# A convolution's written order: taps of the second half ahead of the first half's mean, tap matrices and evictions later

## The chip, the cores and the metric

The kernel runs on one core of one Trainium2 chip. The metric is the device time of one execution in microseconds (us). Five engines take part: TensorE (PE in the profile; PEld is its loading of weights), VectorE (DVE), ScalarE (ACT), GpSimd (POOL), which here mainly issues loads of weights, and SyncE (SP), which issues most DMA transfers.

## The reference

A decoder trunk of two layers for one sequence of 512 positions and 1024 channels. Layer 0 mixes with a state-space group and an attention group, layer 1 with a convolution module; each mixer and each MLP is followed by a residual addition and a layer norm. What matters here is the convolution module of layer 1:

```python
def conformer_conv(x, w_pw1, b_pw1, w_dw, b_dw, ln_g, ln_b, w_pw2, b_pw2):
    h = x @ w_pw1 + b_pw1                       # 1024 -> 2048
    val, gate = jnp.split(h, 2, axis=-1)
    h = val * jax.nn.sigmoid(gate)
    h = lax.conv_general_dilated(               # causal, 31 taps, each channel by itself
        h, w_dw[:, None, :], window_strides=(1,), padding=[(CONV_SIZE - 1, 0)],
        dimension_numbers=('NWC', 'WIO', 'NWC'), feature_group_count=CONV_WIDTH) + b_dw
    h = jax.nn.silu(layer_norm(h, ln_g, ln_b))  # norm over the 1024 channels
    return h @ w_pw2 + b_pw2
...
x = layer_norm(DEEPNORM_ALPHA * x + mix, ln1_g[layer], ln1_b[layer])
ffn = sqrelu_mlp(x, ffn_w1[layer], ffn_b1[layer], ffn_w2[layer], ffn_b2[layer])
```

## The kernel before, in words

Activations lie with channels on the partitions: eight channel tiles of 128 by 512 positions. A float32 product is three products on TensorE (high by high, low by high, high by low), so every operand is split into `whi`, `wlo` or the like: ScalarE makes the high part and VectorE the low one. Layer norms go over partitions: a product with a matrix of `ones` (`colmean`, L959) gives a mean or a variance to all partitions. They go by halves of the sequence, positions 0 to 255 and 256 to 511.

The convolution module follows layer 0's MLP and its norm (tiles `xbh`, `xbl`; the first products with them are named `pl`). For each of the eight tiles j, `glu_tile` makes the two products (`pv`, `pg`), ScalarE the sigmoid (`csg`), VectorE the gated tile `hp` (L398). Then come the 31 taps. Tiles 0 to 2 have them all on VectorE (`taps_dve`: one `scalar_tensor_tensor` each, in turn into `cy` and `cz`, which an addition at the end joins). Tile 3 has 11 taps on TensorE and 19 on VectorE; ScalarE opens `cy` and `cz`. Tiles 4 to 7 have all on TensorE: `weights_4` makes matrices W from the tap weights on VectorE (L1184), `spread` copies `hp` four times, shifted, into tiles `H` by DMA (L1192, on SP's queue), and `taps_128` multiplies (`cw`, L1200, four column groups at once). ScalarE then evicts the result into `cy` with the bias. The sum over tiles, for the mean, grows in `sc` (`LN.add`), one addition by VectorE for each tile and half.

The norm over channels is in three steps: `centred` (the mean `mpc`, subtraction on VectorE, squares `sqc` on ScalarE, their sums on VectorE), `scaled_var` (the variance `vpc`, then the reciprocal root on ScalarE and three steps on VectorE), and `normalised` (for each tile: a product on VectorE, Silu on ScalarE, and the split into `csh` by ScalarE and `csl` by VectorE). What follows is the tail: the products with `w_pw2` (`tld`, 24 of them for a tile and half, in `Tail.run`), added to the residual `X` by VectorE, with the sum `sd` for the next norm. After it come that norm (`mpd`, `vpd`, `xdh`, `xdl`) and the first products of the last MLP (`fl`).

What sets the order is a list written by hand, `CONV_ORDER` (L39). Each word is a step: a letter, the tile, and a third character for the half (0 or 1) where a step does only one.

- `g` is `glu_tile`, `u` its value product alone, `h` the copies, `w` the tap matrices, `p` taps on TensorE
- `v` is a part of a tile's taps on VectorE; `PARTS` says that a whole tile has 10 parts and a half has 4
- `f` is eviction and sum of a tile that TensorE has done
- `x` scales the residual, `M`, `Q` and `n` are the three steps of the norm (`n` for two tiles at a time)
- `t` is one tile of the tail

`run` executes the words, and `in_order` chains the instructions that each issues on TensorE, VectorE and ScalarE to those before, so that these three engines run in the order of the list. DMA issues are not chained; SP's and POOL's queues keep the order in which the program was recorded. Tail tiles that the list doesn't name are issued by `tail_norm_lead` after it, and the scheduler places them.

Of the kernel before, what the change touches and what calls it, by code (L numbers as in the profile page):

```python
# [35 lines left out]
CONV = 31  # L36
PE_BLOCKS = (0, 0, 0, 3, 8, 8, 8, 8)
PARTS = (10, 4)
CONV_ORDER = ("w3 w4 g0 v0 v0 g1 v0 v0 v0 v0 v0 g2 v0 w5 v0 v0 v1 g3 h3 v1 v1 v1 v1 g4 h40 h41 v1 v1 x0 v1 w6 v1 v1 g5 h50 w7 p3 p40 h51 "  # L39
              "v20 v20 v20 v20 g6 h60 f40 v30 p50 v30 f50 g70 h70 p41 h61 f41 v30 v30 p60 f60 p70 f70 u71 M0 g71 h71 v21 p51 Q0 p61 f51 p71 f61 "  # L40
              "n0 n0 n0 n0 f71 v21 t v21 t v21 v31 t v31 t v31 v31 t M1 Q1 n1 n1 n1 n1").split()
SPLIT_TILES = 1
ROOM = 288
HP = (0, 1, 2, 3, 0, 1, 4, 5)
# [159 lines left out]
def kernel(ctx: ExitStack, tc: tile.TileContext, a: dict, out: bass.AP):  # L204
# [806 lines left out]
    class Tail:  # L1011
# [7 lines left out]
        def run(self, n):  # L1019

            nj = KT // len(self.xk)
            for _ in range(n):
                h, j = divmod(self.done, KT)
                c0, c1 = HALVES[h]
                ps = nps(f"tl{self.ln.n}{c0}{j}")
                last = gemm(ps, self.ws[j // nj], slice((j % nj) * P, (j % nj + 1) * P), self.xk, c0, c1)
                x = X[j][:, c0:c1]
                if self.bias is None:
                    tt(x, ps[:, c0:c1], x, ALU.add)
                else:  # L1030
                    stt(x, ps[:, c0:c1], self.bias[:, j : j + 1], x, ALU.add, ALU.add)
                self.ln.add(j, X, c0, c1)
                self.done += 1
            return last
# [283 lines left out]

    split_at = CONV_ORDER.index("t")
    run(CONV_ORDER[:split_at])  # L1320

    def the_rest(t):
        run(CONV_ORDER[split_at:], t)

# [197 lines left out]
```

## Time and profile before

| | |
|---|---|
| median of 3 runs (lowest, highest) | 1161.32 us (1161.25, 1162.76) |
| profiled execution, its own time | 1162.09 us |
| its span, first to last instruction | 1160.4 us |
| mean granted TensorE clock | 0.992 |
| TensorE busy | 1130.9 us, 97% |
| VectorE busy | 810.6 us, 70% |
| ScalarE busy | 538.1 us, 46% |
| DMA | 175.35 MB, mean 151 GB/s |

The convolution lies between about 632 us (the end of the norm ahead of it) and 813 us (the first `fl` behind its tail). Times in a row of the profile are in us from the span's start. A row of the timeline has the start, the length, the engine, the line, the operation with its tiles and shapes, how many, and in brackets how long the engine was idle before it and who ended that. Rows of a stretch give the length, then for each engine the busy time and the number of instructions, then the granted TensorE clock (1.00 is full speed), the DMA engines' share and GB/s.

### The profile page before, as it was taken

To read this page: it belongs to the slowest core of one execution; us is meant where nothing else is said; L and a number is where in the kernel's file an instruction comes from. 1 tells how busy PE (TensorE), PEld (TensorE's weight loads), DVE (VectorE), ACT (ScalarE), POOL (GpSimd) and SP (SyncE) were. 2 spreads that over 40 slices of the span, in tenths; PEclk is the share of its full clock that TensorE was granted. 3 is DMA by queue.
4 is the path that set the end of the run, shared out by engine and by line. 5 is a ranking of instruction groups with operands and counts; after the bars stand their busy time and mean duration, and the time that the engine had idled before them with its cause. 6 is when DMAs were issued, how large, how long until landed. Compare 5 with 4: busy or idle time off the path is not lost.

```text
span 1160.4 us, 16446 instructions
## 1 busy us (share of the span) xinstructions
PE 1130.9 (97%) x6460; PEld 949.7 (82%) x6460; DVE 810.6 (70%) x1408; ACT 538.1 (46%) x814; POOL 39.7 (3%) x77
## 2 busy tenths in 40 slices
PE   9999999999999999999999999988999999999997
PEld 7777777799888888888899877688988888888885
DVE  7998875498646545645548887697795958588337
ACT  6956778345525424524403221515674536363530
POOL 1000000000000000000011210002000000000000
PEclk9999999999999999999999999999999999999999
DMA  9621221242787877788426785345024141514211
GB/s 203 171 66 51 70 77 58 91 145 69 231 280 264 269 275 263 265 301 293 146 81 211 243 269 168 101 145 185 34 90 129 56 149 41 172 37 154 66 53 73
DMA packets 152109, 175.35 MB, mean 151 GB/s; under 512 B 15522, under 2 KB 124834, under 8 KB 152032
## 3 DMA queue, kind: packets, MB, share of 16 engines
q1 hardware_dynamic: 143232, 142.81, 38.7%
q0 software_dynamic: 8640, 31.46, 8.0%
q8 instruction: 51, 0.84, 0.3%
q14 instruction: 26, 0.21, 0.1%
q10 hardware_dynamic: 160, 0.03, 0.0%
HBM read 132.25 MB, written 35.65 MB: 145 GB/s over the span
## 4 chain that ended last, share of the span: by engine, by line
PE 83%; DMA 6%; DVE 5%; ACT 4%; issue 2%; SPq 0%; DVEq 0%; ACTq 0%
PE f L265 21%; PE acf L265 11%; PE s L1407 10%; PE fl L265 5%; PE tld L265 4%; PE h L1452 4%; PE tlb L265 4%; PE pv L265 3%; PE pg L265 3%; DMA raw<-in_ffn_w_dram 3%; PE cw L1200 2%; PE tla L265 2%; PE acmo L265 2%; PE pl L265 2%; PE v L265 1%
## 5 line engine op out<-in xcount | busy, mean ns | idle before, releaser
L117 ACT CAST whi<-raw 128x1024 fp32r<-128x1024 f32 (+1 forms) x150 | 156.8, 1061 | 260.9 <-PE acf L265 68.8
L118 DVE TENSOR_TENSOR wlo<-raw,whi 128x1024 fp32r<-128x1024 f32 (+1 forms) x150 | 183.7, 1236 | 123.2 <-ACT whi L117 123.0
L265 PE MATMUL f<-xah,whi 128*128 128x512 f32 x208 | 81.1, 390 | 0.0
L265 PE MATMUL f<-xal,whi 128*128 128x512 f32 x208 | 81.1, 390 | 0.0
L265 PE MATMUL f<-xah,wlo 128*128 128x512 f32 x208 | 80.9, 389 | 0.0
L265 PE MATMUL f<-xdh,wlo 128*128 128x512 f32 x208 | 80.9, 389 | 0.0
L265 PE MATMUL f<-xdh,whi 128*128 128x512 f32 x208 | 80.9, 389 | 0.0
L265 PE MATMUL f<-xdl,whi 128*128 128x512 f32 x208 | 80.9, 389 | 0.0
L265 PE MATMUL acf<-hh,whi 128*128 128x512 f32 x192 | 75.9, 396 | 0.0
L265 PE MATMUL acf<-hh,wlo 128*128 128x512 f32 x192 | 75.5, 393 | 0.0
L265 PE MATMUL acf<-hl,whi 128*128 128x512 f32 x192 | 75.2, 392 | 0.0
L1407 PE MATMUL s<-whi,al 128*128 128x512 f32 x168 | 65.0, 390 | 0.0
L1407 PE MATMUL s<-wlo,ah 128*128 128x512 f32 x168 | 64.9, 389 | 0.0
L1407 PE MATMUL s<-whi,ah 128*128 128x512 f32 x168 | 64.5, 392 | 0.0
L118 DVE TENSOR_TENSOR wlo<-quad,whi 128x1536 fp32r<-128x1536 f32 x28 | 49.1, 1754 | 7.5 <-ACT whi L117 7.4
L117 ACT CAST whi<-quad 128x1536 fp32r<-128x1536 f32 x28 | 41.0, 1483 | 17.0 <-PE f L265 8.0
L398 DVE SCALAR_TENSOR_TENSOR cy<-hp,wdw,cy 128x256 f32<-128x256 f32 (+1 forms) x80 | 46.2, 577 | 0.9 <-ACT cy L192 0.9
L265 PEld LDWEIGHTS f<-xah,wlo 128*128 128x128 f32 x208 | 39.0, 188 | 8.2
L265 PEld LDWEIGHTS f<-xah,whi 128*128 128x128 f32 x208 | 39.0, 188 | 8.2
L265 PEld LDWEIGHTS f<-xdh,whi 128*128 128x128 f32 x208 | 39.1, 188 | 8.1
L265 PEld LDWEIGHTS f<-xdh,wlo 128*128 128x128 f32 x208 | 39.1, 188 | 8.1
L265 PEld LDWEIGHTS f<-xdl,whi 128*128 128x128 f32 x208 | 39.1, 188 | 8.0
(649 smaller groups left out, 2986.8 us busy)
## 6 DMA issues: line engine op xcount, KB each, us to landing
raw<-in_ffn_w_dram SPq DMA_DIRECT2D x35, 1024.0 KB, 6.6
kepth<-whi SPq DMA_DIRECT2D x30, 512.0 KB, 3.1
keptl<-wlo SPq DMA_DIRECT2D x30, 512.0 KB, 3.1
whi<-kepth POOLq DMA_DIRECT2D x30, 512.0 KB, 4.0
wlo<-keptl POOLq DMA_DIRECT2D x30, 512.0 KB, 5.2
raw<-in_ffn_w_dram SPq DMA_DIRECT2D x28, 512.0 KB, 4.0
raw<-in_conv_w_pw_dram SPq DMA_DIRECT2D x12, 1024.0 KB, 6.9
quad<-in_ffn_w_dram SPq DMA_DIRECT2D x16, 768.0 KB, 4.1
```

What stands on the lines that cost most here:

```text
L117: i0 = nc.scalar.copy(hi, raw).ins
L118: i1 = nc.vector.tensor_sub(lo, raw, hi.bitcast(F32)).ins
L265: ins = PE.matmul(ps[:, c0:c1], u[:, k, ksl], v[:, c0:c1], start=start and k == 0 and i == 0, stop=stop and k == n - 1 and i == 2).ins
L398: V.scalar_tensor_tensor(o, x, s, y, op0=op0, op1=op1)
L1200: PE.matmul(cps[j, c0][32 * g : 32 * g + 32, c0:c1], Ws[j][:, 4 * b + g, :], Hs[j, c0][g][:, 4 * b : 4 * b + c1 - c0], start=b == 0, stop= ...
L1407: PE.matmul(ps, u, v[:, p, :], start=chain == i and p == 0 and n_ == 0, stop=p == len(As) - 1 and n_ == 2, skip_group_check=True)
L1452: PE.matmul(ps, u, v, start=k == 0 and i == 0, stop=k == nb_last - 1 and i == 2)
```

## The change

The table of words is written anew; nothing else is.

```diff
-CONV_ORDER = ("w3 w4 g0 v0 v0 g1 v0 v0 v0 v0 v0 g2 v0 w5 v0 v0 v1 g3 h3 v1 v1 v1 v1 g4 h40 h41 v1 v1 x0 v1 w6 v1 v1 g5 h50 w7 p3 p40 h51 "
-              "v20 v20 v20 v20 g6 h60 f40 v30 p50 v30 f50 g70 h70 p41 h61 f41 v30 v30 p60 f60 p70 f70 u71 M0 g71 h71 v21 p51 Q0 p61 f51 p71 f61 "
-              "n0 n0 n0 n0 f71 v21 t v21 t v21 v31 t v31 t v31 v31 t M1 Q1 n1 n1 n1 n1").split()
+CONV_ORDER = ("g0 w3 v0 v0 g1 v0 v0 v0 v0 v0 v0 g2 v0 v0 v1 v1 g3 h3 v1 v1 v1 v1 v1 w4 g4 h40 h41 v1 v1 x0 v1 w5 w6 g5 h50 p3 p40 h51 "
+              "v20 v20 v20 v20 v30 v30 f40 v30 g6 h60 w7 v30 p50 f50 v21 v21 g70 h70 p41 h61 f41 v21 p60 v21 f60 p70 v31 f70 u71 v31 M0 g71 h71 v31 p51 Q0 p61 p71 "
+              "n0 n0 n0 n0 f51 f61 v31 t t f71 t t M1 t t Q1 n1 n1 n1 n1").split()
```

The steps are the same ones, and each does what it did. The four parts of `v21` and two of `v31` stand ahead of `M0`, a third behind it; before, one of `v21` stood behind `M0`, and all others behind `n0`. The matrices `w3` and `w4` follow `g0` and the taps of tile 1 instead of opening the list, and `w5` and `w7` stand later too. The evictions `f51` and `f61` stand behind `n0`, which they stood ahead of. `M1` comes after four tail tiles and `Q1` after six. On TensorE the order up to the first tail tile is the old one.

On VectorE, around the gated first half of tile 7 (`hp5`, step `g70`), whose copies `h70` TensorE waits for; `cy2` and `cz0` are tile 2's accumulators, `cy3` and `cz1` tile 3's, `sc0` and `sc256` the sums of the two halves. Before:

```order
L398 SCALAR_TENSOR_TENSOR cy3_6697<-hp3_6158,wdw_3268,cy3_6697 128x256
L394 TENSOR_TENSOR sc0_6473<-sc0_6473,cy5_6742 128x256
L1175 MEMSET hp5_6160 128x31
L398 SCALAR_TENSOR_TENSOR hp5_6160<-pv70_6749,PV_88,csg70_6799 128x256
L394 TENSOR_TENSOR sc256_6475<-sc256_6475,cy4_6694 128x256
L398 SCALAR_TENSOR_TENSOR cz1_6162<-hp3_6158,wdw_3268,cz1_6162 128x256
L398 SCALAR_TENSOR_TENSOR cy3_6697<-hp3_6158,wdw_3268,cy3_6697 128x256
```

The same place now:

```order
L398 SCALAR_TENSOR_TENSOR cz0_6161<-hp2_6157,wdw_3268,cz0_6161 128x256
L398 SCALAR_TENSOR_TENSOR cy2_6593<-hp2_6157,wdw_3268,cy2_6593 128x256
L398 SCALAR_TENSOR_TENSOR cz0_6161<-hp2_6157,wdw_3268,cz0_6161 128x256
L1175 MEMSET hp5_6160 128x31
L398 SCALAR_TENSOR_TENSOR hp5_6160<-pv70_6775,PV_88,csg70_6825 128x256
L394 TENSOR_TENSOR sc256_6472<-sc256_6472,cy4_6639 128x256
L398 SCALAR_TENSOR_TENSOR cy2_6593<-hp2_6157,wdw_3268,cy2_6593 128x256
```

Ahead of `hp5` stand 14 taps of tile 2's second half (the last three are shown) and all of tile 3's first half; before, half of that tile's taps came after it.

On ScalarE, between the squares of the first half and its Silu (`rc0` is the reciprocal root, `cw` the taps of a tile on TensorE). Before:

```order
L198 ACTIVATE csg7256_7010<-pg7256_6931,PV_88 128x256
L194 ACT_TABLE_LOAD
L198 ACTIVATE rc0_7062<-vpc0_7057,cb_85 128x256
L192 ACTIVATE cy5_6742<-cw5256_7024,PV_88 128x256
L192 ACTIVATE cy6_6891<-cw6256_7085,PV_88 128x256
L194 ACT_TABLE_LOAD
L198 ACTIVATE cy0_6182<-cy0_6182,PV_88 128x256
L255 CAST csh0_7069<-cy0_6182 128x256
```

Now:

```order
L198 ACTIVATE csg7256_7050<-pg7256_6966,PV_88 128x256
L194 ACT_TABLE_LOAD
L198 ACTIVATE rc0_7100<-vpc0_7095,cb_85 128x256
L194 ACT_TABLE_LOAD
L198 ACTIVATE cy0_6180<-cy0_6180,PV_88 128x256
L255 CAST csh0_7107<-cy0_6180 128x256
```

The two evictions are gone from between root and Silu; they follow the last cast of the first half.

On TensorE, around the second half's mean `mpc256`, and its variance `vpc256`; `tld0` and a digit is a tail tile of the first half, `tld256` and a digit of the second. Before:

```order
L265 MATMUL tld07_7535<-csh7_7083,wlo145_7210 128x256
L959 MATMUL mpc256_7406<-sc256_6475,ones_76 128x256
L959 MATMUL vpc256_7436<-sqc2560_7409,ones_76 128x256
L959 MATMUL vpc256_7436<-sqc2562_7415,ones_76 128x256
L959 MATMUL vpc256_7436<-sqc2564_7421,ones_76 128x256
L959 MATMUL vpc256_7436<-sqc2566_7427,ones_76 128x256
L265 MATMUL tld2560_7578<-csh0_7069,whi138_6481 128x256
```

Now, first at the mean:

```order
L265 MATMUL tld03_7352<-csh7_7121,wlo141_6772 128x256
L959 MATMUL mpc256_7379<-sc256_6472,ones_76 128x256
L265 MATMUL tld04_7409<-csh0_7107,whi142_7233 128x256
L265 MATMUL tld04_7409<-csl0_7108,whi142_7233 128x256
L265 MATMUL tld04_7409<-csh0_7107,wlo142_7234 128x256
```

The mean stood behind all eight tail tiles of the first half, with the variance directly behind it; it now stands behind the fourth (`tld03`), and the four products of `vpc256` follow the sixth (`tld05`), with two tail tiles of the first half behind them.

## The prediction

> **What bounds the kernel now.** I read the page's busy shares first, then TensorE's (PE's) own waits, then the busy time by stage, then the chain of waits, and last the time lines of VectorE (DVE) and the DMA queue at the places that move. The page's head says that PE is the bound:
>
> ```profile
> span 1160.4 us, 16446 instructions
> ...
> PE 1130.9 (97%) x6460; PEld 949.7 (82%) x6460; DVE 810.6 (70%) x1408; ACT 538.1 (46%) x814; POOL 39.7 (3%) x77
> ```
>
> An edit that adds and removes no arithmetic can therefore only win where PE waits or runs slowly. PE's waits from 625 to 830 us (engine, line, whom it waited for; us in total, times, longest) all lie around the convolution:
>
> ```profile
> PE tld L265 <- ACT csh L255: 3.5, 1, 3.5
> PE vpc L959 <- DVE sqc L394: 3.2, 1, 3.2
> PE pl L265 <- ACT xbh L192: 1.6, 1, 1.6
> PE mpc L959 <- DVE sc L394: 0.8, 1, 0.8
> ```
>
> Four stretches show what lies between (length, busy time of PE, PEld, DVE, ACT, POOL, then granted clock, DMA share, GB/s). The first is the convolution up to its first mean, the second the first half's eight tail products, the third the second half's norm, the fourth the second half's eight tail products:
>
> ```profile
> 643.10:731.80 88.70, 88.70 (x697) 69.20 (x696) 72.58 (x137) 17.00 (x28) 13.94 (x27) 1.00 0.72 225
> 747.10:775.60 28.50, 28.05 (x196) 25.27 (x192) 26.06 (x68) 6.29 (x15) 0.00 (x0) 0.94 0.23 83
> 775.60:787.50 11.90, 4.42 (x12) 2.77 (x11) 8.85 (x25) 6.99 (x14) 0.00 (x0) 0.85 0.55 155
> 787.50:812.90 25.40, 25.40 (x197) 25.29 (x198) 20.51 (x57) 14.60 (x32) 6.37 (x12) 0.94 0.62 221
> ```
>
> The chain of waits (start, us, what) gives a measure for what these tail products need:
>
> ```profile
> 717.76 10.50 PE cw L1200 x192
> ...
> 738.22 1.92 PE vpc L959 x8
> ...
> 743.83 0.47 ACT cy L192
> ...
> 744.32 1.28 ACT L194
> ...
> 745.61 0.61 ACT cy L198
> ...
> 746.25 0.41 ACT csh L255
> ...
> 777.21 2.73 DVE cy L394 x8
> ...
> 787.48 9.94 PE tld L265 x69
> ...
> 804.39 8.63 PE tld L265 x72
> ```
>
> The last row is 72 products in 8.63 us, 0.12 us each, so a tile of 24 needs 2.88 us and a half (192) 23.0 us. The first half took 28.5: an excess of 5.5 us. The second took 25.4, with two row sums of about 0.3 us inside: an excess of 1.8. The third stretch holds a mean (0.3) and a variance (1.92, row 738.22), so 9.7 of its 11.9 us is loss. Finer stretches show what part of the excess is the clock (seventh number, after the five engines):
>
> ```profile
> 748.00:752.00 4.00, 3.63 (x14) 2.07 (x14) 3.28 (x10) 3.84 (x10) 0.00 (x0) 1.00 0.00 0
> 752.00:756.00 4.00, 3.92 (x16) 3.19 (x17) 3.31 (x10) 1.58 (x4) 0.00 (x0) 0.64 0.00 0
> 756.00:760.00 4.00, 4.00 (x34) 4.00 (x33) 4.00 (x12) 0.00 (x0) 0.00 (x0) 0.93 0.00 0
> ...
> 788.00:792.00 4.00, 4.00 (x26) 4.00 (x25) 3.26 (x9) 3.87 (x9) 0.00 (x0) 0.67 0.00 0
> ```
>
> In the first, 14 products ran where 33 would fit: PE is fed one channel tile at a time by ScalarE (ACT) and DVE. Behind it, and again behind the norm, the granted clock falls: 0.36 and 0.07 of 4 us lost the first time, 1.7 us, and 0.33 of 4 us, 1.3, the second.
>
> **The change part by part.** *Tap matrices out of the MLP's norm.* DVE's time line in the last norm ahead of the convolution:
>
> ```profile
> 631.76 0.42 DVE L398 SCALAR_TENSOR_TENSOR tb<-vpb,rb 128x256 f32<-128x256 f32 x1 [1.60 <-ACT rb L198]
> 632.10 0.55 DVE L1184 TENSOR_TENSOR W<-mask,w 128x384 f32<-128x384 f32 x1
> 632.57 0.42 DVE L394 TENSOR_TENSOR tb<-tb,rb 128x256 f32<-128x256 f32 x1
> 632.90 1.22 DVE L1184 TENSOR_TENSOR W<-mask,w 128x1024 f32<-128x1024 f32 x1
> 634.04 0.42 DVE L398 SCALAR_TENSOR_TENSOR rb<-tb,rb 128x256 f32<-128x256 f32 x1
> ...
> 823.29 0.42 DVE L398 SCALAR_TENSOR_TENSOR td<-vpd,rd 128x256 f32<-128x256 f32 x1 [1.60 <-ACT rd L198]
> 823.75 0.43 DVE L394 TENSOR_TENSOR td<-td,rd 128x256 f32<-128x256 f32 x1
> ```
>
> Two matrices stand between three steps that PE waits for. The steps start 2.28 us apart (631.76 to 634.04); with nothing between they start 0.46 apart (823.29, 823.75), so 0.92. PE starts 1.35 us earlier and its 1.6 us wait shrinks to 0.25: **-1.35**. The matrices go to places where DVE waits anyway.
>
> *More DVE work ahead of the copies of tile 7.* Ahead of the first mean come 38 taps of the second half (29 of tile 2, 9 of tile 3). DVE has 88.7 - 72.6 = 16.1 us idle in the first stretch; the taps only need tiles that are long there. The place where it hurts is the gated tile `hp5` (step g70), whose copies (h70) TensorE's taps p70 wait for:
>
> ```profile
> 672.60 0.75 DVE L398 SCALAR_TENSOR_TENSOR cz<-hp,wdw,cz 128x512 f32<-128x512 f32 x1
> 673.26 0.75 DVE L398 SCALAR_TENSOR_TENSOR cy<-hp,wdw,cy 128x512 f32<-128x512 f32 x1
> ...
> 680.82 0.75 DVE L398 SCALAR_TENSOR_TENSOR hp<-pv,PV,csg 128x512 f32<-128x512 f32 x1 [2.14 <-ACT csg L198]
> ...
> 709.05 0.75 DVE L398 SCALAR_TENSOR_TENSOR hp<-pv,PV,csg 128x512 f32<-128x512 f32 x1 [0.64 <-ACT csg L198]
> ...
> 718.37 0.48 DVE L398 SCALAR_TENSOR_TENSOR hp<-pv,PV,csg 128x256 f32<-128x256 f32 x1 [4.13 <-ACT csg L198]
> ...
> 753.27 0.43 DVE L256 TENSOR_TENSOR csl<-cy,csh 128x256 fp32r<-128x256 f32 x1 [0.52 <-ACT csh L255]
> ...
> 754.78 0.48 DVE L398 SCALAR_TENSOR_TENSOR cz<-hp,wdw,cz 128x256 f32<-128x256 f32 x1
> 755.17 0.48 DVE L398 SCALAR_TENSOR_TENSOR cy<-hp,wdw,cy 128x256 f32<-128x256 f32 x1
> ```
>
> Between g3 and g70 the new order has 24 more narrow taps (0.396 us apart: 9.5), three fewer wide ones (0.66: -2.0), two more matrices (1.14 each: 2.3) and an addition with its sum (about 1.0): 10.8 us more. Idle there were 2.14 + 0.64 + 4.13 = 6.9. So g70 ends at 718.85 - 1.35 - 6.9 + 10.8 = 721.4. Its copies, on SP's queue:
>
> ```profile
> 718.88 5.50 SPq L1192 DMA_DIRECT2D H<-hp  x8
> ...
> DMA to landing us min/median/max: 2.9/3.0/3.1
> ```
>
> Eight issues in 5.5 us; the fourth, the last that p70 needs, starts some 2.1 us after the first and lands 3.0 later, 5.1 in all: 726.5. p70 is the last third of row 717.76, due at 724.75 - 1.35 = 723.4. PE waits **+3.0** us (taken range 2 to 3.5), a stall that did not exist. Everything on PE up to the tail then stands 1.65 us later than before. The sum for the first mean is no later: it needs p70's eviction, and DVE is through its taps by then. SP's copies h61, queued behind h70, land some 3 us after it, and p61 is due at 741.8, behind the variance (738.2 + 1.9 + 1.65). The copies h71 have the first weight load of the MLP next on SP; it no longer waits for tile 2's taps and may share the DMA engines with them, half a microsecond on p71 at worst, which the next term's wait absorbs.
>
> *ScalarE's evictions behind the normalisation.* Today ACT runs 743.83 (the eviction of p61, held until PE had made it), then the table load, then the first Silu at 745.61. Without evictions the load follows the variance's root. That root moves with PE by +1.65 to about 741.8; load to 743.6, DVE's three steps and product to 744.15, Silu and cast to 745.2, against 746.66 today: 1.45 us earlier, while PE arrives at 748.8 instead of 747.1. The last `csl` comes at 753.7 - 1.45 = 752.25 (row 753.27), the first tail tile ends at 752.6 instead of an unstarved 751.65: excess 1.0 in place of 5.5, clock loss included: **-4.5**.
>
> The Trainium skill, "ScalarE: Activation LUTs", section "What ACT_TABLE_LOAD costs", gives 1283 ns for the load and about 1380 ns of drain with every switch. The trace agrees on the load (1.28) and has Silu at 745.61 directly behind it; by the page's sum the first Silu would come 0.85 us later and the gain be smaller by that.
>
> *The second mean inside the tail.* PE's order now has the mean behind four tail products and the variance behind six. From the last `csl` DVE needs three sums, five taps, an addition with its sum and two tail additions, about 5.1 us, while PE does three more tiles in 8.6. From the mean to the variance's input it needs the fourth tail addition, 2.7 us of subtractions (row 777.21) and the last squares, some 4.6 us, under two tiles of 5.75: a margin of 1.1 us. Root, load and first cast take 3.7 us more, under the two last tiles. Nothing of the 9.7 us is left: **-9.7**. If that cover fails, this term is what comes back, up to 3.5 us of it.
>
> *The second half's tail.* With PE never idle 3 us, the clock stays up; 0.4 us of starvation remain of 1.8: **-1.4**.
>
> Sum: -1.35 + 3.0 - 4.5 - 9.7 - 1.4 = -14.0 (rounded). The profiled execution took 1162.09 us (1160.4 of span), 0.77 over the median of 1161.32; the same difference against the median gives **1147.3 us**. Behind the tail the engines' orders are the old ones but for a few places in PE's, so the MLP starts as much earlier as the tail ends.
>
> **The rivals.** *The clock still falls.* The first fall came after a stretch in which PE was busy 3.63 of 4 us, with many short waits and no long one. The 3.0 us stall at p70, or the first tail tile, can bring it on: 1.7 or 3.4 us, so 1149.0 or 1150.7. For it: row 752.00. Against it: the wait of 1.6 us at `pl` left no slow stretch behind. The Trainium skill, "TensorE: Matmul & The Clock Gate", section "What's actually happening", has half rate follow an idle window of about 3.4 us; by that rule neither stall does it, and row 752.00 shows that starvation without such a gap does.
>
> *The second mean is late.* If DVE's 1.1 us margin goes, PE waits ahead of the variance: up to 3.5 us, 1150.8.
>
> *No stall at p70.* If the copies land earlier (g70 less late), 3.0 comes off: 1144.3.
>
> *DVE has no room (slower).* If the moved work (38 taps, 15.0; their addition and sum, 0.9; two matrices, 1.6: 17.5 us) finds no idle time ahead of the first mean, PE, in order, waits there: +17.5 - 1.35 + 1.7 (clock) - 4.5 - 9.7 - 1.4 = +2.3, 1163.6. It decides from 15.3 of the 17.5 on. Against it: 16.1 us of idle time, ended by ACT's gates and evictions for which these taps have no need.
>
> *Given back later.* If the last MLP is paced by its weight loads and not by the tail's end, all returns: 1161.3. Against it: those loads wait for buffers of the convolution, which come free earlier too.
>
> **How the numbers follow.** Forecast 0.60; clock 0.18; late mean 0.08; no stall 0.08; slower 0.03; given back 0.03. The best imaginable, all of 1.35 + 5.5 + 9.7 + 1.8 gone and no stall, is 18.4 less: 1143. The range is 1143.5 to 1151.5: from nearly that to a late mean with a little clock loss. About 0.2% (2.3 us) is what a measurement can tell from no change: faster 0.94, same 0.03, slower 0.03.
>
> **What would show it.** Right: PE's wait for `xbh` near 0.25 us; PE waiting 2 to 3.5 us ahead of one group of `cw`; the mean `mpc` of the second half between tail products, with no PE wait for `sc` or `sqc`; granted clock 1.00 from 748 to 812. Wrong: a PE wait for `sc` ahead of the first mean, an idle PE ahead of the second variance, or a tail that ends earlier and an MLP that does not.

## The result and the profile after

The changed kernel takes 1147.57 us (median of 4 executions, 1146.98 to 1149.69) against 1161.78 for the kernel before in the same rounds (4 executions, 1161.25 to 1162.76): a ratio of 0.988, interval 0.9863 to 0.9897, or 14.2 us less. The forecast was 1147.3, 14.0 less. Timed a second time, the ratio was 0.9886 (0.9869 to 0.9903).

The head of the page of the changed kernel, and PE's waits from 620 to 815 us:

```profile
span 1145.3 us, 16443 instructions
...
PE cw L1200 <- DMA H<-hp: 1.1, 3, 0.5
PE pl L265 <- ACT xbh L192: 0.3, 1, 0.3
```

The waits for `csh` (3.5), `sqc` (3.2) and `sc` (0.8) are gone, the one for `xbh` is down from 1.6 to 0.3, and a new one for the copies `H` has come. The spans differ by 15.1 us, more than the medians do, so the first thing to settle is where the changed stretch begins. In the chain of waits of the kernel before, two rows mark its ends: the variance of the last norm ahead of the convolution, and the first product of the MLP behind the tail:

```profile
630.78 0.45 PE vpb L959 x2
...
813.02 3.00 PE fl L265 x25
```

The same chain after the change (start, us, what):

```profile
629.21 0.45 PE vpb L959 x2
...
632.65 0.74 PE pl L265 x4
...
714.84 6.58 PE cw L1200 x117
721.42 3.13 DMA H<-hp
...
724.59 3.64 PE cw L1200 x58
728.23 3.06 PE pv L265 x24
...
743.12 0.41 ACT csh L255
...
750.15 0.44 DVE csl L256
...
750.63 9.14 PE tld L265 x74
759.77 0.43 PE mpc L959 x2
760.20 5.75 PE tld L265 x48
765.95 1.73 PE vpc L959 x8
767.68 12.45 PE tld L265 x99
...
797.89 2.88 PE fl L265 x24
```

`vpb` starts 1.57 us earlier than in the execution of before. That is not the change: in the nine profiled executions of this study it starts anywhere from 627.36 to 633.05, and the changed kernel itself, profiled twice, has it at 629.21 and at 628.37. So the ruler for the change is the length from `vpb` to `fl`: 182.24 us before (813.02 - 630.78), 168.68 after, **13.56 us less**. With 1.57 from ahead of it, that makes up the 15.1 of the spans. All steps below are measured from `vpb`, and this takes out the offset. The table has this length for every kernel here:

```
kernel                               vpb      fl       length   against its parent
before                               630.78   813.02   182.24
changed                              629.21   797.89   168.68   -13.56 (before)
changed, second profile              628.37   796.91   168.54
tap matrices alone (E1)              627.36   807.71   180.35   -1.89 (before)
evictions in front (E2)              630.34   803.45   173.11   +4.43 (changed)
mean behind seven tiles (E3)         633.05   808.02   174.97   +6.29 (changed)
early mean, late taps (E4)           628.67   813.93   185.26   +3.02 (before)
gate of tile 7 earlier (E5)          627.88   794.50   166.62   -2.06 (changed)
gate of tile 7 later (E6)            629.37   802.45   173.08   +4.40 (changed)
```

VectorE's time line after the change, at the three places that the forecast leaned on: the gate of tile 7, the last sum ahead of the second mean, and the last squares ahead of the second variance:

```profile
719.02 0.45 DVE L398 SCALAR_TENSOR_TENSOR hp<-pv,PV,csg 128x256 f32<-128x256 f32 x1
...
755.42 0.42 DVE L394 TENSOR_TENSOR sc<-sc,cy 128x256 f32<-128x256 f32 x1
...
763.26 1.42 DVE L394 TENSOR_TENSOR sqc<-sqc,sqc 128x256 f32<-128x256 f32 x4
```

The last sum is there at 755.84 and PE asks for it at 759.77; the last squares end at 764.68 and PE asks at 765.95. Two stretches of 4 us (PE, PEld, DVE, ACT, POOL, then granted clock, DMA share, GB/s), at the new stall and behind the first tail tile:

```profile
720.00:724.00 4.00, 3.35 (x42) 1.30 (x34) 4.00 (x11) 0.47 (x1) 0.00 (x0) 1.00 0.66 157
...
752.00:756.00 4.00, 4.00 (x35) 4.00 (x34) 3.73 (x10) 0.00 (x0) 0.00 (x0) 1.00 0.35 82
```

The clock, 0.64 in the second of these stretches before, is 1.00 in both.

### The profile page after: what moved, and what is told of

Read it like the earlier page. It is cut to its first block, busy times and chain, and to the rows that moved or that the text cites. A ratio compares the mean times of both kernels' runs of the same rounds, so it can differ in the third digit from the quotient of the medians.

```text
span 1145.3 us, 16443 instructions
## 1 busy us (share of the span) xinstructions
PE 1124.8 (98%) x6460; PEld 945.5 (83%) x6460; DVE 811.6 (71%) x1408; ACT 538.7 (47%) x814; POOL 39.7 (3%) x77
## 4 chain that ended last, share of the span: by engine, by line
PE 88%; DVE 4%; DMA 4%; ACT 3%; issue 1%; SPq 0%; DVEq 0%; ACTq 0%
PE f L265 24%; PE acf L265 11%; PE s L1407 10%; PE fl L265 6%; PE tlb L265 4%; PE tld L265 4%; PE h L1452 4%; PE pv L265 3%; PE pg L265 3%; PE cw L1200 2%; PE tla L265 2%; PE pl L265 2%; PE v L265 1%; PE acmo L265 1%; DMA raw<-in_mix_w_in_dram 1%; PE gg L265 1%
## 5 line engine op out<-in xcount | busy, mean ns | idle before, releaser
L265 PEld LDWEIGHTS f<-xal,whi 128*128 128x128 f32 x208 | 39.0, 188 | 8.1
```

Of the source, the lines that this page charges most:

```text
L265: ins = PE.matmul(ps[:, c0:c1], u[:, k, ksl], v[:, c0:c1], start=start and k == 0 and i == 0, stop=stop and k == n - 1 and i == 2).ins
```

## The experiments

Theory: five terms, as in the prediction. Rivals: the time comes from one place alone (the mean's place in PE's order, or the taps' place), the new stall is one of the DMA queue and not of VectorE's order, or the clock makes the difference. Each kernel below edits only the written order; all ratios are to the kernel before in the same rounds.

**E1: the tap matrices alone.** Kernel before with

```
-"w3 w4 g0 v0 v0 g1 ... g2 v0 w5 v0 ... v1 v1 v1 v1 g4 ... x0 v1 w6 v1
+"g0 w3 v0 v0 g1 ... g2 v0 v0 ... v1 v1 v1 v1 w4 g4 ... x0 v1 w5 w6 v1
```

> The kernel before with one part of the change alone: the four tap matrices (w3, w4, w5, w7's pair left) stand where the new order has w3, w4, w5 and w6; all else as before. Theory (matrices out of the last norm's steps): PE's wait for xbh falls from 1.6 to about 0.25 us, the convolution starts 1.35 us earlier and so does the end: 1.35 us below before, ratio 0.9988; everything from the first mean on keeps its waits (3.2 ahead of vpc, 3.5 ahead of tld). Rival (the first mean and the tail are paced by DVE, not by PE's start): PE's wait goes but comes back ahead of the first mean; 0.0 us, ratio 1.000. Rival (most of the gain came from here): over 4 us.

Measured: 1158.59 us against 1161.22, ratio 0.9981 (0.9971 to 0.9991). PE's waits, and the resumed `pl` in its chain:

```profile
PE tld L265 <- ACT csh L255: 3.5, 1, 3.5
PE vpc L959 <- DVE sqc L394: 3.2, 1, 3.2
PE mpc L959 <- DVE sc L394: 0.8, 1, 0.8
PE pl L265 <- ACT xbh L192: 0.3, 1, 0.3
```

```profile
630.80 0.74 PE pl L265 x4
```

From the variance (627.36) to the resumed `pl` it is 3.44 us, against 4.79 before (635.57 - 630.78): -1.35, to the hundredth the term. The other waits are unchanged. The remaining 0.54 of the trace's 1.89 lies behind the first mean (from `pl` to that mean both take 95.8 us), in stretches that both kernels run in part at a lowered clock: 0.25 in the first half's tail, 0.14 in `vpc` (3.69 before, 3.55 here) and 0.11 in the `tld` row behind it (9.94 and 9.83). The edit changes no order there, so it is not put down to the edit. The timed interval (1.0 to 3.4 us) holds 1.35 and excludes both rivals.

**E2: the evictions back in front of the normalisation.** Changed kernel with

```
-p51 Q0 p61 p71 n0 n0 n0 n0 f51 f61 v31 t t
+p51 Q0 p61 f51 p71 f61 n0 n0 n0 n0 v31 t t
```

> The changed kernel with f51 and f61 put back in front of n0. Theory: ACT holds the eviction of p61 until PE has made it (about 743.7 in the changed kernel's profile), then the table load of 1.28 and the first Silu at about 745.5 instead of 742.5: the last csl and the first tail tile end 3.0 us later, and starvation of the first tile brings the clock down for another 1.7: 3.0 to 4.7 us above the changed kernel, ratio to before 0.9905 to 0.992. Rival (the evictions' place costs nothing, since DVE's steps of the norm hold Silu anyway): ratio 0.988. On the clock: if starvation with short waits lowers it, the row behind the first tile shows about 0.64; if only an idle window of over 3 us does, it stays at 1.00.

Measured: 1151.20 us, ratio 0.9911 (0.9897 to 0.9924). Its chain at the place, and two stretches behind the first tail tile:

```profile
744.90 0.47 ACT cy L192
745.39 1.28 ACT L194
...
746.68 0.61 ACT cy L198
...
754.34 0.44 DVE csl L256
...
754.82 10.53 PE tld L265 x74
```

```profile
752.00:756.00 4.00, 3.78 (x14) 2.63 (x15) 3.13 (x9) 2.60 (x6) 0.00 (x0) 0.83 0.01 3
756.00:760.00 4.00, 4.00 (x28) 4.00 (x27) 2.30 (x6) 0.00 (x0) 0.00 (x0) 0.75 0.48 137
```

The eviction, the table load and the first Silu stand in a row again. The last `csl` ends 124.44 us behind `vpb` instead of 121.38: +3.06. Behind it the same 74 products take 10.53 us instead of 9.14: +1.39, at a clock of 0.83 and 0.75. Together 4.45, the 4.43 of the ruler; by the ratios it is about 3.6 us (0.9911 - 0.988). So the term is shown in both its halves: the order on ScalarE, and the clock that its starvation brings down. In the row with 0.83, 14 products ran where 33 fit; in the changed kernel nothing of the kind happens.

**E3: the second mean behind seven tail tiles.** Changed kernel with

```
-t t f71 t t M1 t t Q1 n1 n1 n1 n1
+t t f71 t t t t t M1 Q1 n1 n1 n1 n1
```

> The changed kernel with the second half's mean and variance behind seven tail tiles instead of four and six; all taps stand where the change has them. Theory: from the mean to the first csl of the second half runs a chain of about 11 us, of which mean, variance and one tail tile (0.4 + 1.7 + 2.9) are PE work; the rest, 6.0 us, becomes PE waiting, and 1.3 us of clock may follow: 6.0 to 7.3 us above the changed kernel, ratio to before 0.9930 to 0.9945. Rival (early taps gain by themselves, the mean's place does not matter): no more than 1 us above the changed kernel, 0.988 to 0.989.

Measured: 1152.75 us, ratio 0.9923 (0.9910 to 0.9935). PE's waits, and two stretches at the start of the second half's tail:

```profile
PE tld L265 <- ACT csh L255: 3.5, 1, 3.5
...
PE vpc L959 <- DVE sqc L394: 0.7, 1, 0.7
```

```profile
780.00:784.00 4.00, 2.57 (x12) 2.57 (x13) 2.88 (x8) 3.53 (x8) 0.00 (x0) 0.53 0.00 0
784.00:788.00 4.00, 4.00 (x24) 4.00 (x24) 2.76 (x8) 3.88 (x9) 0.00 (x0) 0.62 0.02 4
```

Although every tap stands early, the wait for `csh` is back in full (3.5), and of the 4.0 for `sqc` and `sc` 0.7 is left. In the trace the total is as expected (+6.29); by the ratios it is about 5 us (0.9923 - 0.988), under the expected 6.0 to 7.3, and the traced execution has the lowest clock of the six (0.993, the others 0.995 to 0.997), so the trace may show more than the usual loss. The parts are not as expected: 4.2 us of waiting, not 6.0, and the 2.1 that are left, in rows with a clock of 0.53 and 0.62, instead of 1.3. So most of the term hangs on the mean's place. What the early taps gain by themselves is not shown: one tail tile still stands behind the mean here, and its 2.9 us may cover most of the 3.3 us of waiting that do not come back.

**E4: the early mean without the early taps.** Kernel before with

```
-v31 t v31 t v31 v31 t M1 Q1 n1 n1 n1 n1
+v31 t v31 t v31 v31 M1 t t Q1 n1 n1 n1 n1
```

> The kernel before with one part of the change alone: the second half's mean behind four tail tiles and its variance behind six, while all taps stay where they were, behind the first half's norm. Theory (the mean can only move because its taps moved): VectorE has the last sum for the mean at about 774.4 in before's times, PE reaches the mean at about 764 and waits some 10 us for sc; then two tiles, variance and two tiles cover the rest, and the second half's tail starts at about 788 against 787.5: within 2 us of before, ratio 0.999 to 1.002. Rival (the mean's place in PE's order is what gains, wherever the taps stand): 9.7 us below before, ratio 0.9915.

Measured: 1163.14 us against 1160.02, ratio 1.0024 (1.0013 to 1.0036): slower than before. Its waits, two rows of its chain, and the clock:

```profile
PE mpc L959 <- DVE sc L394: 10.5, 1, 10.5
```

```profile
772.79 1.22 PE mpc L959 x2
774.01 7.98 PE tld L265 x48
```

```profile
748.00:752.00 4.00, 3.69 (x13) 2.17 (x14) 2.94 (x9) 3.40 (x8) 0.00 (x0) 0.96 0.00 0
752.00:756.00 4.00, 4.00 (x24) 4.00 (x23) 4.00 (x11) 0.00 (x0) 0.00 (x0) 0.61 0.00 0
...
760.00:764.00 4.00, 2.28 (x20) 2.07 (x18) 3.93 (x11) 0.00 (x0) 0.00 (x0) 1.00 0.12 10
764.00:768.00 4.00, 0.00 (x0) 0.00 (x0) 3.93 (x11) 0.00 (x0) 0.00 (x0) 0.67 0.97 338
768.00:772.00 4.00, 0.00 (x0) 0.00 (x0) 3.96 (x11) 0.00 (x0) 0.00 (x0) 0.50 0.63 242
...
776.00:780.00 4.00, 4.00 (x24) 4.00 (x24) 2.93 (x9) 2.67 (x5) 0.00 (x0) 0.63 0.97 264
```

PE reaches the mean and stands for 10.5 us, as the theory had it, while VectorE is busy without a break: it still has the taps to do. What the mean saves behind it is paid in front of it. The 3.0 us beyond that are clock: the mean's row and two tiles take 9.20 us here (1.22 + 7.98) and 6.18 in the changed kernel (0.43 + 5.75). The expectation (0.999 to 1.002) had no price for that and was missed by it. With E3: the mean's early place gains nothing without the early taps, and without that place 6.3 us of the gain are lost; the taps make room, the mean uses it.

**E5 and E6: the place of tile 7's gate on VectorE.** Changed kernel with one part of `v21` (seven taps) fewer, and one more, in front of g70 and h70:

```
-v21 v21 g70 h70 p41 h61 f41 v21 p60 v21 f60
+v21 g70 h70 v21 p41 h61 f41 v21 p60 v21 f60        (E5)
+v21 v21 v21 g70 h70 p41 h61 f41 p60 v21 f60        (E6)
```

> The changed kernel with g70 and h70 in front of the second part of v21 (seven taps, 2.8 us of DVE) instead of behind it. Theory (the copies of tile 7 are late because DVE gates the tile late): the copies land about 2.5 us earlier, PE's stall ahead of the last third of cw falls from 2.9 to about 0.4 us, and 2.3 us of it reach the end: about 1145.3 against 1147.6, ratio to before 0.986. Rival (DVE is the bound up to the first mean, so the wait only moves to mpc or vpc): PE then waits for sc or sqc, ratio 0.9875 to 0.988. Rival (the landing is set by the DMA queue and not by the gate): the stall stays, ratio 0.988.

> The changed kernel with g70 and h70 behind a third part of v21 (seven taps, 2.8 us of VectorE) instead of two. Theory (VectorE's place of the gate sets the landing): the stall ahead of the last third of cw grows from 2.9 to 5.7 us and all of it reaches the end: 2.8 us above the changed kernel, ratio to before 0.990 to 0.991. Rival (the stall is of the DMA queue): as the changed kernel, 0.988. On the clock: if an idle stretch of over 3.4 us lowers it, the row behind the stall falls below 1.00 and 1.3 to 1.7 us more are lost (ratio 0.992); if it takes starvation in many short waits as in the tail, it stays at 1.00.

E5 measured: 1144.99 us, ratio 0.9855 (0.9841 to 0.9870), the fastest kernel here. PE's waits from 620 to 830 us have one row left, `xbh` with 0.3, and the first mean's row in the chain is a little long:

```profile
727.64 0.70 PE mpc L959 x2
```

The mean starts 99.76 us behind `vpb`, not 102.09 as in the changed kernel (its chain has it at 731.30): 2.33 us of the stall are gone. The row's 0.70 instead of 0.43 is what the first rival said, in small: VectorE, now the last to be ready, holds PE for 0.27 us. That leaves -2.06. The interval of the ratio lies below both rivals (0.9875 and more).

E6 measured: 1149.32 us, ratio 0.9905 (0.9890 to 0.9920); the changed kernel in the same rounds 1146.11. Gate, wait, chain and clock:

```profile
721.95 0.44 DVE L398 SCALAR_TENSOR_TENSOR hp<-pv,PV,csg 128x256 f32<-128x256 f32 x1
```

```profile
PE cw L1200 <- DMA H<-hp: 3.3, 1, 3.3
```

```profile
722.42 2.74 DMA H<-hp
725.30 7.50 PE cw L1200 x64
```

```profile
724.00:728.00 4.00, 2.70 (x14) 1.12 (x18) 3.93 (x11) 0.00 (x0) 0.00 (x0) 0.55 0.54 137
728.00:732.00 4.00, 4.00 (x50) 2.75 (x45) 0.73 (x2) 0.00 (x0) 0.00 (x0) 0.60 0.01 4
```

The gate ends 93.02 us behind `vpb` instead of 90.26: +2.76, the seven taps. `p70` ends 103.43 behind it instead of 99.02: +4.41, so 1.65 us more are lost, at a clock of 0.55 and 0.60. The landing follows the gate, earlier and later: SP issues the first copy within 0.1 us of the gate's end in E5 (715.4 behind 715.36), in the changed kernel (719.5 behind 719.47) and in E6 (722.42 behind 722.39). The DMA queue does not set it. The timed gain of the changed kernel over E6 is 3.2 us, less than the trace's 4.40. The four timed executions have spans of 1147.0, 1147.1, 1148.1 and 1149.8, with a mean clock of 0.997 in the first two and 0.995 in the others, so the fall may not come every time; only one of the four has a trace, and this stays open.

## Why the prediction was right

*Tap matrices.* Forecast -1.35; from `vpb` to `pl` 3.44 after, 4.79 before: -1.35, and E1 has the same alone.

*Stall at tile 7.* Forecast +3.0. From 714.84 to 728.23 the group takes 13.39 us, 10.50 before: +2.89. On the ruler, the gate was forecast to end at 90.6 (721.4 - 630.78) and the copies to land at 95.7; they did at 90.26 and 95.34 (724.55). The step that reads idle time, added taps and queue from rows held. One reading of it was too simple: the wait does not show as one of 2 to 3.5 us. PE does a few products with each copy that lands, so the view of waits shows 1.1 us in three pieces, and only the chain's start times show all of it. E5 and E6 move it both ways.

*Evictions.* Forecast: `csh` of tile 0 at 114.4 on the ruler, the last `csl` at 121.5, first tile 1.0 us over 2.88. Measured 114.32 (743.53) and 121.38 (750.59). PE's time line has the first and the 24th product of the first tail tile, after the change:

```profile
747.08 0.39 PE L265 MATMUL tld<-csh,whi 128*128 128x256 f32 x1
...
750.85 0.28 PE L265 MATMUL tld<-csh,wlo 128*128 128x256 f32 x1
```

and before it:

```profile
747.12 0.39 PE L265 MATMUL tld<-csh,whi 128*128 128x256 f32 x1
...
754.13 0.42 PE L265 MATMUL tld<-csh,wlo 128*128 128x256 f32 x1
```

From start to start that is 3.77 us against 7.01: 3.24 of the 4.5. The rest is the clock behind the tile, 1.00 now. E2 gives 3.06 and 1.39 for the two. The table load now ends at 741.92 and Silu starts at 742.49, 0.02 us behind VectorE's product: ScalarE no longer holds it up.

*Second mean in the tail.* Forecast -9.7, a margin of 1.1 us. No wait for `sc` or `sqc`; the margin was 1.27 (764.68 to 765.95). E4 shows that the place gains nothing without the taps, E3 that 6.3 us of the gain hang on the place.

*Second half's tail.* Forecast 0.4 us of starvation left. The 99 products of the last long `tld` row would take 11.88 at 0.12 each and take 12.45: 0.57.

The tail, from its first product to `fl`, takes 50.81 us (747.08 to 797.89), 65.90 before (747.12 to 813.02): -15.09, forecast -15.6. So -1.35 + 2.89 - 15.09 = -13.55, the ruler's 13.56 but for rounding. On the ruler the forecast's -14.0 was 0.4 us too good: 0.5 too good in the tail, 0.1 too bad at the stall. That the medians come within 0.3 us of the forecast is in part luck: the interval of the ratio allows gains from 12.0 to 15.9 us.

*The rivals.* The clock did not fall at the stall (1.00 from 720 to 724), and the margin of the second mean held. But the chance of 0.18 for the first was not too high: E6, with 2.8 us more, has it. "No room on VectorE", put at 0.03, was nearer than that: E5 shows VectorE as the last to be ready for the first mean as soon as the stall is gone. The 16.1 us of idle time that the forecast counted were there, but nearly all of them are used: from 640.18 to 728.88, as long a stretch, VectorE is idle for 1.4 us now. Nothing was given back later: `fl` starts 15.13 us earlier and the span ends 15.1 us earlier.

On the clock, the Trainium skill ("TensorE: Matmul & The Clock Gate", section "What's actually happening") has half rate follow an idle window of some 3.4 us that runs freely. The traces agree in part: in E6 and E4 the clock falls 2.4 and 3.1 us into a wait (worked out in the last section). That the two differ fits a free window, but both falls come sooner than a window of 3.4 us that is idle throughout could end. A free window would also fit that E6's executions differ, which no trace here shows. E2 does not come under that sentence: it had no such gap. The Trainium skill ("TensorE: Matmul & The Clock Gate", section "A second HAM failure mode: psum-queue depth-cycling") tells of falls by frequent short idling, without a size; E2's row gives one, 14 products where 33 fit.

## What to carry to other kernels

A reduction in the middle of a PE-bound stage costs the whole chain behind it unless other PE work stands there to cover it, and that work can only be put there if what feeds the reduction is finished earlier: move the feeding work into idle time of its engine first, then the reduction. Here the reduction's move alone cost time (E4), and without it 6.3 us of the gain were lost (E3). Each step moved ahead pushes back what stands behind it on that engine: look there for the operation whose result goes out by DMA, and put it in front. Before a span's difference is put down to a change, measure both executions from the last point ahead of it.

## What the runs showed of the hardware

- PE's granted clock falls in two ways. Inside one long wait: in E4 PE is idle from 762.3; the clock halves (0.50 in row 768 to 772), so the 0.67 of row 764 to 768 puts the fall at 765.4, 3.1 us later. In E6 PE is idle from 722.0 (725.30 less 3.3), and the 0.55 of row 724 to 728 puts the fall at 724.4, 2.4 us later. And without one: 13 or 14 products in 4 us where 33 fit (E4's row 748 to 752, E2's row 752 to 756) are followed by 0.61 and 0.75. A stall of 2.9 us with products in between (changed kernel) left it at 1.00.
- It comes back late: in E4 PE resumes at 772.79, and row 776 to 780 with 0.63 puts the return at about 779.0, 6.2 us later, worked out in the same way; in E6 it resumes at 725.30, and the 0.60 of row 728 to 732 puts the return at 731.2, 5.9 us later. So E4's wait of 10.5 us costs 3.0 more.
- Seven of the profiled executions have the same instructions up to `vpb` and reach it anywhere from 627.36 to 633.05: 5.7 us, more than any single edit above is worth in the trace but E3's. Most of it arises between 560 and 600 us, where PE has 290 products in E1 and 252, at a clock of 0.96, in E3; what decides this, no run here shows.
